# Two buffers for the keys of a differential attention, a tile of their own for the sample keys, and a smaller DMA scratch

## The chip, the core and the metric

The kernel runs on one core of one Trainium2 chip. TensorE (PE) multiplies matrices, VectorE (DVE), ScalarE (ACT) and GpSimd (POOL) do the rest, and SyncE (SP) issues every transfer of the program on one queue. The metric is the device time of one execution in microseconds, the median of the runs shown.

## The reference

One step of a one-layer hybrid encoder on a prompt of 2048 tokens and a sample of 32 tokens with a cache of 128 past tokens. All data is float32; the width is 1024.

```python
qa, ka, va, qb, kb, vb = split_proj(rmsnorm(hp, g_attn[i]), w_in[i])
oa = diff_attn_prompt(qa, ka, va, t5_table, lam)        # 4 heads, two q/k maps of 64, values of 128
ob = band_attn_prompt(qb, kb, vb, band_table[i])        # 8 heads of 64, 8 chunks of 64 back
hp = hp + merge(oa, ob, subln_g[i], out_norm_b[i], w_out[i], lam_init)
hp = ffn_ple(hp, p_prompt[i], g_mlp[i], w_up[i], w_down[i], w_ple_gate[i], w_ple_proj[i])
...
def diff_core(q, k, v, bias, mask, lam):
    s = jnp.einsum('bqhmd,bkhmd->bhmqk', q, k).astype(jnp.float32) * (HEAD_DIM ** -0.5) + bias[:, None]
    s = jnp.where(mask, s, NEG)
    p = jax.nn.softmax(s, axis=-1)
    w = p[:, :, 0] - lam * p[:, :, 1]
    return jnp.einsum('bhqk,bkhe->bqhe', w.astype(v.dtype), v)
```

The sample goes through the same layer; its keys in the differential attention are the 128 cached ones and its own 32. The mask is causal by chunks of 64 tokens. The outputs are both hidden states after a last norm, and the new keys and values.

## The kernel before

Large products are done in float32r in three terms: each operand is split into a rounded part and the rest (`split`, line 160 on; `mm3`, lines 186 to 192), so that one product of two operands is three matmuls. Tokens go in four blocks of 512; the last one takes the 32 sample tokens along.

Queries, keys and values are projected first (`proj`) and written to DRAM: `qS`, `kS`, `vS`. `kS` holds for each head the 2048 prompt keys, then 128 cached, then 32 sample keys: 2208 columns (`KC`), as a rounded part and a rest. The attention reads them back.

`attn_a` is the differential attention. It is called with a list of query pairs `js`; pair j is the 256 queries from 256 j on, and 8 stands for the sample. The calls are `JA0 = [(0, 1), (2, 3)]` early, in the pool `a0` (`self.small`, key tiles of 1024 columns), and `JA1 = [(4, 5), (6, 7, 8)]` later, in the pool `a1`. Each call goes over four heads g. For each head it loads

- a bias tile `ba` (`bias_a`, one buffer, with a memset on GpSimd for the mask),
- a key tile `ka` (one buffer): for each of two halves of the partitions, pieces of 1024 columns, so 2, 4 or 6 transfers,

and then runs the pairs (`attn_a_pair`). A pair loads its query tile `q` (`load_q`, two buffers, four transfers), and for each of its two 128-query tiles computes scores `s` with two matmuls (line 567) per key block of up to 512 columns and map, takes the maximum on VectorE (line 573, or with the bias line 576), the exponential on ScalarE (line 581), combines the two maps (lines 603, 604), transposes the weights on TensorE (`tpp`, line 639) and multiplies them with the values `v` (`o`, lines 653 to 655). `ka`, `ba` and `q` of the next head or pair can be loaded into a buffer only when the last reader of its old contents is done.

Nothing of the order is written by hand: a scheduler of the framework orders all instructions of each engine at build time, by program order as priority and by its own model of times and of free buffers. So work of other stages stands between the instructions of the attention: the projections of the band attention in the first stage, and in the second the output projection, the MLP (`ups`, `dps`) and the gate of the first two token blocks. Those run while `a1` is open because their tiles and those of `a1` lie side by side in SBUF. SP issues transfers strictly in its order and waits before each for what that transfer needs.

At address 0 of SBUF, 16384 bytes of each partition are set aside by default as scratch for dynamic DMAs (`dynamic_dma_scratch_size`); all pools lie behind it.

Of the kernel before, what the change touches and what calls it, by code (L numbers as in the profile page):

```python
# [13 lines left out]
F32R = mybir.dt.float32r  # L14
# [5 lines left out]
P = 128  # L20
D = 1024
SP = 2048
SS = 32
T = SP + SS
PAST = 128
KC = SP + PAST + SS
# [107 lines left out]
class Kern:  # L134
# [376 lines left out]
    def attn_a(self, js, pool, ps_s, ps_t, ps_o):  # L511
        nc = self.nc
        last = 8 in js
        nk = KC if last else 256 * (js[-1] + 1)
        for g in range(4):
            ba = self.bias_a(pool, g)
            kt = pool.tile([P, 2, 1024 if self.small else KC], F32R, tag="ka", bufs=1, name="ka")
            for hl in range(2):
                src = self.kS[g, hl].rearrange("(m r) c -> r m c", m=2)
                for c0 in range(0, nk, 1024):  # L520
                    c1 = min(c0 + 1024, nk)
                    self.dma(kt[64 * hl : 64 * hl + 64, :, c0:c1], src[:, :, c0:c1])
            for j in js:
                self.attn_a_pair(g, j if j < 8 else None, kt, ba, pool, ps_s, ps_t, ps_o)

    def attn_a_pair(self, g, j, kt, ba, pool, ps_s, ps_t, ps_o):
        nc = self.nc
# [7 lines left out]
        q = self.load_q(pool, g, t0, nq, (0, 1))  # L535
        ws = []
        for qi, t in enumerate(tiles):
            if samp:
                nr = SS
                blocks = [(SP, PAST + SS, 0)]  # L540
                kb = SP
                nkeys = PAST + SS
            else:
                nr = P
                kb = 0
                nkeys = P * (t + 1)
                nfar = max(nkeys - 256, 0)
                nb = (nfar + 511) // 512
                blocks = []
                pos = 0  # L550
                for i in range(nb):
                    n = P * ((nfar // P - pos // P + nb - i - 1) // (nb - i))
                    blocks.append((pos, n, None))
                    pos += n
                blocks.append((nfar, nkeys - nfar, 256 - (nkeys - nfar)))
            nb = len(blocks)
            e = [
                pool.tile([P, 2048 if not self.small else 1024], F32, tag=f"e{m}", bufs=2 if m == 0 or self.small else 1, name="e")
                for m in range(2)
            ]  # L560
            nm = pool.tile([P, 2, 8], F32, tag="nm", bufs=2, name="nm")
            z = pool.tile([P, 2, 8], F32, tag="z", bufs=2, name="z")
            for bi, (k0, n, near) in enumerate(blocks):
                for m in range(2):
                    s = ps_s.tile([P, 512], F32, tag="s", name="s")[:nr, :n]
                    for hl in range(2):
                        nc.tensor.matmul(  # L567
                            s, q[:, m, hl, P * qi : P * qi + nr], kt[:, m, k0 : k0 + n], start=hl == 0, stop=hl == 1
                        )
                    dst = e[m][:nr, k0 - kb : k0 - kb + n]  # L570
                    nmx = nm[:nr, m, bi : bi + 1]
                    if near is None:
                        nc.vector.tensor_reduce(nmx, s, axis=AX.X, op=ALU.max, negate=True)  # L573
                        src = s
                    else:
                        nc.vector.tensor_tensor_reduce(
                            dst, s, ba[:nr, near : near + n], 1.0, -3e38, ALU.add, ALU.max, nmx
                        )
                        nc.vector.tensor_scalar(nmx, nmx, -1.0, None, op0=ALU.mult)
                        src = dst  # L580
                    nc.scalar.activation(dst, src, AF.Exp, bias=nmx, accum_out=z[:nr, m, bi : bi + 1])  # L581
            c = pool.tile([P, 2, 8], F32, tag="c", bufs=2, name="c")
            rz = pool.tile([P, 2], F32, tag="rz", bufs=2, name="rz")
            if nb > 1:
                gm = pool.tile([P, 2], F32, tag="gm", bufs=2, name="gm")
                nc.vector.tensor_reduce(gm[:nr], nm[:nr, :, :nb], axis=AX.X, op=ALU.min)
                for m in range(2):
                    nc.scalar.activation(
                        c[:nr, m, :nb], nm[:nr, m, :nb], AF.Exp, bias=gm[:nr, m : m + 1], scale=-1.0
                    )  # L590
                nc.vector.tensor_tensor(z[:nr, :, :nb], z[:nr, :, :nb], c[:nr, :, :nb], op=ALU.mult)
                nc.vector.tensor_reduce(rz[:nr], z[:nr, :, :nb], axis=AX.X, op=ALU.add)
                nc.vector.reciprocal(rz[:nr], rz[:nr])
                nc.vector.tensor_scalar(c[:nr, 0, :nb], c[:nr, 0, :nb], rz[:nr, 0:1], None, op0=ALU.mult)
                nc.vector.tensor_scalar(
                    c[:nr, 1, :nb], c[:nr, 1, :nb], rz[:nr, 1:2], self.nlam[:nr], op0=ALU.mult, op1=ALU.mult
                )
            else:
                nc.vector.reciprocal(c[:nr, :, 0], z[:nr, :, 0])
                nc.vector.tensor_scalar(c[:nr, 1, 0:1], c[:nr, 1, 0:1], self.nlam[:nr], None, op0=ALU.mult)  # L600
            for bi, (k0, n, near) in enumerate(blocks):
                sl = slice(k0 - kb, k0 - kb + n)
                nc.scalar.activation(e[1][:nr, sl], e[1][:nr, sl], AF.Copy, scale=c[:nr, 1, bi : bi + 1])
                nc.vector.scalar_tensor_tensor(
                    e[0][:nr, sl], e[0][:nr, sl], c[:nr, 0, bi : bi + 1], e[1][:nr, sl], op0=ALU.mult, op1=ALU.add
                )
            ws.append(e[0])
# [7 lines left out]
        for c0 in range(0, len(kts), 4):  # L615
# [16 lines left out]
            for qi, w in enumerate(ws):  # L632
                nr = SS if samp else P
# [14 lines left out]
            for x, (i, kn) in enumerate(ch):  # L648
# [3 lines left out]
                last = c0 + x == len(kts) - 1  # L652
# [653 lines left out]
```

## Time and profile before

| | |
|---|---|
| runs | 3277.6, 3271.13, 3279.51 us |
| median | 3277.6 us |
| profiled execution | 3282.74 us |
| its span, first to last instruction | 3281.0 us |
| mean granted TensorE clock | 0.974 |
| first stage of `attn_a`, 230 to 560 us | PE busy 304.8 of 330 us |
| second stage of `attn_a`, 1331 to 2131 us | PE busy 762.2 of 800 us |

A row such as `PE s L567 <- DMA ka<-kS: 10.9, 5, 4.2` says that PE stood idle before the matmul of line 567 that writes `s`, until a transfer into `ka` had landed: 10.9 us in 5 cases, the longest 4.2 us. In a timeline, a row gives start, length, engine, line, operation, output and inputs, and in brackets the idle time before it with what ended it. In a table of windows each engine has its busy time and number of instructions; the last three columns are the granted clock, the busy share of the DMA engines and what they moved in GB/s.

### The profile page before, as it was taken

The page shows a single profiled execution, that of the slowest core. Times are in us where ns is not written, and L with a number is a line of the kernel's source. Part 1 is how long each engine was busy: PE and PEld are TensorE (multiplying, and loading weights), DVE is VectorE, ACT ScalarE, POOL GpSimd, SP SyncE. Part 2 cuts the span into 40 slices and gives each one's busy share as a digit, 9 for nine tenths or more (in the row PEclk, how much of TensorE's full clock was granted, in tenths as well). Part 3 has the DMA queues.
Part 4 walks back from the last instruction along what each step waited for, and adds up shares of the span by engine and source line. Part 5 has one row for each costly group of instructions (what it writes and reads, how often), then busy time and mean ns, then how long its engine had stood idle before and what let it go on. Part 6 is the DMA issues. An engine that isn't in the chain of part 4 may idle for free.

```text
span 3281.0 us, 51609 instructions
## 1 busy us (share of the span) xinstructions
PE 3096.6 (94%) x17881; PEld 2713.4 (83%) x17881; DVE 1562.2 (48%) x3952; ACT 1696.1 (52%) x3717; POOL 1711.0 (52%) x2515
## 2 busy tenths in 40 slices
PE   6998999899989999999999999998989999999998
PEld 6877788899877888778788877877779999999988
DVE  5116786444455544566655655735442232223235
ACT  4226676666656766666665656744442222222245
POOL 5436776433335544656654644676954333333377
PEclk9998999999999999999999999999989999999999
DMA  7488886876778654545655355357531111111123
GB/s 230 169 258 241 226 246 199 230 225 199 221 210 240 166 140 120 159 137 152 195 136 142 109 139 139 111 159 227 164 102 49 46 46 50 45 48 46 46 91 106
DMA packets 519085, 489.03 MB, mean 149 GB/s; under 512 B 37884, under 2 KB 414016, under 8 KB 518824
## 3 DMA queue, kind: packets, MB, share of 16 engines
q1 hardware_dynamic: 518824, 485.73, 50.8%
q8 instruction: 142, 2.33, 0.3%
q14 instruction: 119, 0.97, 0.1%
HBM read 379.06 MB, written 110.49 MB: 149 GB/s over the span
## 4 chain that ended last, share of the span: by engine, by line
PE 54%; DMA 5%; DVE 4%; POOL 2%; ACT 1%; issue 1%; SPq 0%; DVEq 0%; POOLq 0%; ACTq 0%
PE dps L190 7%; PE ups L191 7%; PE ups L190 7%; PE ups L192 7%; PE dps L192 7%; PE dps L191 7%; PE s L567 2%; PE gps L190 1%; PE gps L191 1%; DMA ka<-kS 1%; PE gps L192 1%; PE tpp L639 1%; POOL wl L164 1%; DMA wr<-w_up 1%; PE ob L766 1%
## 5 line engine op out<-in xcount | busy, mean ns | idle before, releaser
L164 POOL TENSOR_TENSOR wl<-wr,wh 128x256 fp32r<-128x256 f32 x936 | 690.9, 770 | 501.1 <-ACT wh L169 473.0
L971 DVE TENSOR_TENSOR h<-h,dps 128x512 f32<-128x512 f32 (+1 forms) x640 | 373.1, 585 | 597.5 <-PE dps L192 584.9
L169 ACT ACTIVATE wh<-wr 128x1024 fp32r<-128x1024 f32 x338 | 356.9, 1056 | 581.0 <-PE dps L191 285.7
L154 POOL TENSOR_TENSOR wl<-wr,wh 128x256 fp32r<-128x256 f32 x416 | 305.0, 764 | 407.0 <-ACT wh L169 403.7
L190 PE MATMUL dps<-uh,wh 128*128 128x512 f32 (+1 forms) x1280 | 458.6, 358 | 10.1 <-DVE h L971 5.5
L190 PE MATMUL ups<-cH,wh 128*128 128x512 f32 (+1 forms) x1280 | 453.3, 354 | 9.9 <-ACT relu L936 5.0
L191 PE MATMUL ups<-cL,wh 128*128 128x512 f32 (+1 forms) x1280 | 452.9, 354 | 4.1 <-DVE cL L175 3.6
L192 PE MATMUL ups<-cH,wl 128*128 128x512 f32 (+1 forms) x1280 | 453.2, 354 | 0.0
L191 PE MATMUL dps<-ul,wh 128*128 128x512 f32 (+1 forms) x1280 | 451.0, 353 | 0.0
L192 PE MATMUL dps<-uh,wl 128*128 128x512 f32 (+1 forms) x1280 | 450.9, 353 | 0.0
L154 POOL TENSOR_TENSOR ul<-relu,uh 128x136 fp32r<-128x136 f32 (+1 forms) x320 | 201.7, 652 | 167.7 <-ACT uh L169 166.4
L190 PEld LDWEIGHTS ups<-cH,wh 128*128 128x128 f32 x1280 | 242.8, 190 | 42.3 <-ACT relu L936 5.3
L190 PEld LDWEIGHTS dps<-uh,wh 128*128 128x128 f32 x1280 | 242.5, 189 | 42.4 <-DVE h L971 9.0
L191 PEld LDWEIGHTS ups<-cL,wh 128*128 128x128 f32 x1280 | 243.3, 190 | 36.0 <-DVE cL L175 3.8
L192 PEld LDWEIGHTS dps<-uh,wl 128*128 128x128 f32 x1280 | 242.0, 189 | 33.7
L192 PEld LDWEIGHTS ups<-cH,wl 128*128 128x128 f32 x1280 | 243.1, 190 | 30.1
L191 PEld LDWEIGHTS dps<-ul,wh 128*128 128x128 f32 x1280 | 242.2, 189 | 26.2
L190 PE MATMUL qps<-aH,wh 128*128 128x512 f32 (+1 forms) x640 | 231.3, 361 | 8.6 <-ACT kr L432 3.4
L191 PE MATMUL qps<-aL,wh 128*128 128x512 f32 (+1 forms) x640 | 229.6, 359 | 0.0
L192 PE MATMUL qps<-aH,wl 128*128 128x512 f32 (+1 forms) x640 | 228.9, 358 | 0.0
L567 PE MATMUL s<-ka,q 128*128 128x256 f32 (+4 forms) x784 | 190.4, 347 | 26.6 <-DMA ka<-kS 10.9
L581 ACT ACTIVATE e<-s,nm 128x512 f32<-128x512 f32 (+3 forms) x256 | 155.1, 611 | 68.7 <-DVE nm L573 46.0
(218 smaller groups left out, 7118.3 us busy)
## 6 DMA issues: line engine op xcount, KB each, us to landing
wr<-w_up SPq DMA_DIRECT2D x96, 512.0 KB, 4.2
wr<-w_down SPq DMA_DIRECT2D x96, 512.0 KB, 3.7
wr<-w_in SPq DMA_DIRECT2D x74, 512.0 KB, 5.2
q<-qS SPq DMA_DIRECT2D x256, 128.0 KB, 4.2
v<-vSa SPq DMA_DIRECT2D x64, 512.0 KB, 4.0
ka<-kS SPq DMA_DIRECT2D x32, 512.0 KB, 7.7
wr<-w_out SPq DMA_DIRECT2D x32, 512.0 KB, 5.4
wr<-w_ple_gate SPq DMA_DIRECT2D x32, 512.0 KB, 4.3
```

Source lines behind the costliest of these rows:

```text
L154: nc.gpsimd.tensor_tensor(out[:, sl], a[:, sl], b[:, sl], op=op)
L164: nc.gpsimd.tensor_tensor(out[:, sl], a[:, sl], b[:, sl], op=op)
L169: nc.scalar.activation(hi, raw, AF.Copy)
L190: nc.tensor.matmul(ps, lh, rh, start=start and i == 0, stop=False)
L191: nc.tensor.matmul(ps, lh, rl, start=False, stop=False)
L192: nc.tensor.matmul(ps, ll, rh, start=False, stop=stop and i == n - 1)
L567: nc.tensor.matmul(s, q[:, m, hl, P * qi : P * qi + nr], kt[:, m, k0 : k0 + n], start=hl == 0, stop=hl == 1)
L581: nc.scalar.activation(dst, src, AF.Exp, bias=nmx, accum_out=z[:nr, m, bi : bi + 1])
L639: nc.tensor.transpose(tp[:kn, x, :nr], w[:nr, P * i : P * i + kn], self.ident[:nr, :nr])
L766: nc.tensor.matmul(o[:, qa:qb], vt, pt[:kn, i - kfirst, qa:qb], start=x == 0 and y == 0, stop=x == len(order) - 1 and y == 1,)
L971: nc.vector.tensor_tensor(hv, hv, ps, op=ALU.add)
```

## The change

The key tile `ka` of the differential attention has two buffers where it had one, and in the later stage 2048 columns where it had 2208. The 160 columns that the sample needs go into a small tile `ks` of their own with one buffer, loaded only in the call with the sample; the score matmul subtracts the block base `kb` (0 for prompt pairs, 2048 for the sample) from its column. The scratch for dynamic DMAs shrinks from 16384 to 1024 bytes of each partition. The bytes loaded for the keys are the same. The number of key transfers of a head stays: 2 or 4, and in the call with the sample 4 into `ka` and 2 into `ks` where there were 6 into `ka`.

```diff
     def attn_a(self, js, pool, ps_s, ps_t, ps_o):
         nc = self.nc
         last = 8 in js
-        nk = KC if last else 256 * (js[-1] + 1)
+        nk = SP if last else 256 * (js[-1] + 1)
         for g in range(4):
             ba = self.bias_a(pool, g)
-            kt = pool.tile([P, 2, 1024 if self.small else KC], F32R, tag="ka", bufs=1, name="ka")
+            kt = pool.tile([P, 2, 1024 if self.small else SP], F32R, tag="ka", bufs=2, name="ka")
+            if last:
+                ks = pool.tile([P, 2, PAST + SS], F32R, tag="ks", bufs=1, name="ks")
             for hl in range(2):
                 src = self.kS[g, hl].rearrange("(m r) c -> r m c", m=2)
                 for c0 in range(0, nk, 1024):
                     c1 = min(c0 + 1024, nk)
                     self.dma(kt[64 * hl : 64 * hl + 64, :, c0:c1], src[:, :, c0:c1])
+                if last:
+                    self.dma(ks[64 * hl : 64 * hl + 64], src[:, :, SP:KC])
             for j in js:
-                self.attn_a_pair(g, j if j < 8 else None, kt, ba, pool, ps_s, ps_t, ps_o)
+                self.attn_a_pair(g, j if j < 8 else None, kt if j < 8 else ks, ba, pool, ps_s, ps_t, ps_o)
...
                     for hl in range(2):
                         nc.tensor.matmul(
-                            s, q[:, m, hl, P * qi : P * qi + nr], kt[:, m, k0 : k0 + n], start=hl == 0, stop=hl == 1
+                            s, q[:, m, hl, P * qi : P * qi + nr], kt[:, m, k0 - kb : k0 - kb + n], start=hl == 0, stop=hl == 1
                         )
...
-    nc = bacc.Bacc("TRN2", target_bir_lowering=False, num_devices=1)
+    nc = bacc.Bacc("TRN2", target_bir_lowering=False, num_devices=1, dynamic_dma_scratch_size=1024)
```

## The prediction

> **What bounds the kernel now.** I read the page first, then the waits of PE by stage, then the timeline around the longest waits, then the granted clock in those stretches.
>
> ```profile
> PE 3096.6 (94%) x17881; PEld 2713.4 (83%) x17881; DVE 1562.2 (48%) x3952; ACT 1696.1 (52%) x3717; POOL 1711.0 (52%) x2515
> ```
>
> PE is the bound: 184 us of the 3281.0 us span are without a matmul. The change touches no matmul (17,876 in the built program before and after), so all it can move is those idle stretches and the slower clock after them. The differential attention has two stages: 230 to 560 us (key blocks up to 1024, below "the first stage") and 1331 to 2131 us ("the second stage"). Between its softmax steps the scheduler has put projection matmuls in the first and MLP matmuls in the second. The waits of PE in the second stage (us in total, times, longest):
>
> ```profile
> PE s L567 <- DMA ka<-kS: 10.9, 5, 4.2
> PE s L567 <- issue: 7.2, 2, 4.9
> PE dps L190 <- DVE h L971: 5.5, 6, 1.6
> PE o L653 <- ACT pH L646: 4.5, 4, 2.3
> ```
>
> The score matmuls (line 567) lead the list. The two rows called "issue" are the same wait: both stand at the first score matmul of a head, right behind its key loads. Here is one, on PE and then on SP's queue:
>
> ```profile
> 1893.52 0.28 PE L653 MATMUL o<-pH,v 128*128 128x256 f32 x1
> 1898.72 1.19 PE L567 MATMUL s<-ka,q 128*128 128x512 f32 x2 [4.92 <-issue]
> 1899.71 0.63 PE L190 MATMUL ups<-cH,wh 128*128 128x512 f32 x1
> ```
>
> ```profile
> 1889.55 0.62 SPq L145 DMA_DIRECT2D ka<-kS  x1
> 1890.21 6.06 SPq L145 DMA_DIRECT2D q<-qS  x4
> ```
>
> The one key buffer is free only when the last score matmul of the head before is done; here six key loads and four query loads are then issued, and PE runs out of other matmuls before they land. The seven head changes of the second stage show one such gap each, in order 4.16, 2.29, 0.80, 2.44, 2.51, 4.92 and 0.94 us: 18.1 us, which is 10.9 + 7.2. In the first stage no PE wait names `ka`.
>
> The matmul after the gap takes 0.63 us, where the same shape takes 0.39 to 0.40 before it. The windows from the start of the three costliest gaps to the end of the halved clock (length, PE busy, ..., granted clock, DMA share, GB/s):
>
> ```profile
> 1416.44:1426.73 10.29, 6.13 (x18) 5.13 (x19) 7.40 (x13) 1.61 (x3) 2.55 (x4) 0.67 0.86 199
> 1779.36:1785.12 5.76, 3.25 (x11) 2.80 (x11) 0.69 (x1) 0.79 (x2) 1.40 (x2) 0.70 1.09 201
> 1893.80:1904.60 10.80, 5.88 (x14) 4.66 (x15) 2.31 (x7) 1.31 (x3) 2.77 (x4) 0.68 1.07 226
> ```
>
> All PE work in these windows runs after the gap, at half clock, so half of it is lost: (6.13 + 3.25 + 5.88) / 2 = 7.6 us. Two more key gaps (2.44 and 0.94 us) have a half-clock stretch a little later, but another wait (2.06 and 2.34 us) lies between; 1.7 us each, 3.4 us, I leave to the low end of the range.
>
> **Keys in two buffers: what goes.** In the order of the built program I counted the PE work between the matmul that frees a key buffer and the first score matmul that reads the new keys, at 0.23 us for 128x512 (start to start in the timeline) and in proportion for less. Before, in the second stage, it was 4.6 to 11.4 us at the seven head changes, against landings of the key loads of
>
> ```profile
> DMA to landing us min/median/max: 3.6/7.7/12.3
> ```
>
> After, it is 69 to 117 us there, and 15 to 50 us in the first stage. Even the 12.3 us maximum is covered. So 18.1 us of gaps and 7.6 us of half clock go: -25.7 us. That the other matmuls there are the cover is seen in the count itself; no PE work is added in their place.
>
> **What is late next, second stage.** The other inputs of a head's first score matmul are its query tile, two buffers, four loads of 0.60 us issue each. At the four head changes without a sample block the count between release and use is above 40 us: nothing. At the three that follow the sample block, the buffer comes free only with the last prompt scores of the head before, and the sample block is short: 4.5, 4.2 and 4.5 us, where before it was 15.0, 11.2 and 15.0. The landings of query loads in this stage:
>
> ```profile
> DMA to landing us min/median/max: 2.1/3.9/11.8
> ```
>
> The third load is needed and is issued 1.3 us after the first: 1.3 + 3.9 = 5.2 us at the median, 0.8 us more than the cover, so about 1 us at each change, +3 us. The bounds are 0 and 1.3 + 11.8 - 4.4 = 8.7 us each. I take the median because 11.8 belongs to query loads that stood behind a key burst, and that burst now stands behind them in SP's order. The two sample-key loads of a head carry 160 columns; their one buffer is free after the sample block and their use is above 100 us away, so they cost their issue, 2 x 0.6 us on SP, off the path. At the second of the three changes they stand between the second and third query load; that is within the 3 us.
>
> At the start of the second stage the first keys had 14.0 us of cover and have 11.4; in the trace the first score matmul came 12.3 us after the first key load was issued (1331.7 to 1344.0). Between 0 and 2.6 us; I take +1. Behind those loads on SP now stand the next head's keys, then the attention-output loads and weights of the output projection, as before.
>
> **What is late next, first stage.** The bias tile `ba` keeps one buffer. Its reload waits for VectorE's last use in the head before, and while keys were late too this hardly mattered. Counted in the same way, up to the first matmul that can't run without the biased scores, the cover at the seven head changes is 9.6, 6.3, 7.4, 13.5, 15.8, 3.3 and 9.4 us (before 11.2, 8.2, 4.3, 13.2, 12.6, 18.6 and 13.6). The loads there take
>
> ```profile
> DMA to landing us min/median/max: 2.2/5.1/10.5
> ```
>
> and the masking memset 0.14 us and the add 0.42 us come after: 5.7 us at the median, and some 0.8 us for VectorE to get to the release, my estimate from the two adds in front. So 6.5 us is needed; 3.3 us of cover leaves a gap of 3.2 us, 6.3 us leaves 0.2, and the 3.2 us gap costs 1.7 us of clock (5.76 us at 0.70, above): +5 us. Bounds: 0 (the 4.3 us case before shows no gap above 0.84 us next to it) and, at 10.5 us landings, the second rival below.
>
> **The rest.** The scratch size: the profile has every program transfer on one queue, and nothing of it is issued by POOL, so I cost it at nothing:
>
> ```profile
> q1 hardware_dynamic: 518824, 485.73, 50.8%
> ```
>
> The addresses move, but the attention tiles of the second stage still start 704 bytes above the MLP's tiles that run beside them (before 1728), so no new wait for space. The first 1,234 matmuls and the last 5,432 come in the same order; between them the scheduler has reordered, the same work with the same counts of short covers within a few, and I give that 0, with 5 us either way.
>
> **Sum.** -25.7 + 3 + 1 + 5 = -16.7 us. The profiled execution took 3282.74 us (span 3281.0), 5.1 us above the median; on the median, 3277.6 - 16.7 = 3261 us.
>
> **A rule of the skill.** The trace's row: the 2.51 us gap at 1779.36 is followed by a half-clock window of its own. By the Trainium skill, "TensorE: Matmul & The Clock Gate", Part 1, the clock falls after an idle window of about 3.4 us. By that only the 4.16 and 4.92 us gaps cost clock, 6.0 us in place of 7.6, and a 3.2 us gap in the first stage costs none, so the sum would be -16.8. The measurement differs on the short gap, and the sum goes by it.
>
> **The rivals.** First, nothing is gained: PE has other matmuls and some other wait fills the gaps, as the 5.5 us before `dps` and 4.5 us before `o` do now. For it: only 38 of the stage's 800 us are idle, and the order of what follows a gap changes. Against it: 18.1 of these 38 us stand at exactly the matmul whose cover grows tenfold. 3278 us; chance 0.08.
>
> Second, the bias tile: with all seven loads at 10.5 us, 11.1 us are needed, and the gaps are 1.5, 4.8, 3.7, 0, 0, 7.8 and 1.7 = 19.5 us, with 1.7 us of clock after five of them 28 us: 3277.6 - 25.7 + 4 + 28 = 3284 us. For it: DMA share there is 0.83. Against: the median of 5.1. Chance 0.12.
>
> Third, slower: the query loads after the sample blocks land as late as they did behind key bursts, now because SP holds them behind the sample-key loads, which wait for the sample's scores. 8.7 us at each of three changes, and 3.4 us of clock each (10.29 us at 0.67, above): 36 us, so 3277.6 - 25.7 + 36 + 1 + 5 = 3294 us. It decides from 6.6 us a change on. For it: the order at the second change. Against it: 0.16 MB stand there in place of 2.3 MB. Chance 0.08.
>
> Fourth, the smaller scratch slows each transfer; at 0.1 us for each of 1,639 issues SP gets 164 us more to do, and if a sixth shows, 3289 us. Against it is the queue row above; chance 0.03. The Trainium skill ("DMA: Bandwidth & Descriptors", SWDGE vs HWDGE vs iDMA) puts that scratch on the software path alone.
>
> **The numbers.** The forecast has 0.64; a larger gain 0.05 (no new waits and the 3.4 us as well: -29 us, 3248). A measurement can tell about 0.3%, 10 us. Faster: 0.62 of the forecast and the 0.05, 0.67. Within 0.3%: 0.02 of the forecast, 0.10 of the bias, 0.07 of nothing gained, 0.19. Slower: the rest of these, 0.03, with the third and fourth, 0.14. The range runs from 3246, the larger gain with a little reordering, to 3281, most of the bias case; about 0.2 is outside.
>
> **What would show it.** Right: in the second stage no PE wait on `ka`; at the three changes after a sample block waits of about 1 us on query loads; half-clock stretches near 1420, 1782 and 1898 us gone; in the first stage one gap of about 3 us behind a bias load. Wrong: idle PE time in 1331 to 2131 us still near 38 us, or over 10 us more of it in 230 to 560 us.

## The result: 12 us faster, and the profile after

The changed kernel takes 3265.2 us (median of 12 executions, 3258.5 to 3269.9), the kernel before 3277.3 us in the same round: a ratio of 0.9959, with a 95% interval from 0.9948 to 0.997. That is 12.0 us less; the forecast was 16.7 us less. The profiled execution after took 3263.55 us (span 3261.7, granted clock 0.980, before 0.974). The changed lines push the code down by 4: the score matmul is line 571 now, the residual add `h` line 975, the `o` matmuls lines 657 to 659.

The engine line of the page after: PE is busy 13.5 us less with the same number of matmuls, so part of the gain is clock.

```profile
PE 3083.1 (95%) x17881; PEld 2699.8 (83%) x17881; DVE 1549.0 (47%) x3952; ACT 1693.7 (52%) x3717; POOL 1709.8 (52%) x2515
```

The waits of PE in the second stage, 1331 to 2131 us, after (us in total, times, longest):

```profile
PE dps L190 <- DVE h L975: 8.3, 13, 1.3
PE s L571 <- DMA q<-qS: 3.7, 2, 2.8
PE s L571 <- ACT e L585: 3.2, 2, 2.1
PE o L657 <- ACT pH L650: 2.8, 3, 1.9
PE tpp L643 <- DVE e L608: 2.6, 2, 2.0
```

No row names `ka`, and "issue" behind it is gone too: all 18.1 us of key gaps have left. The list is not simply shorter, though. The MLP's wait for `h` rose from 5.5 us in 6 cases to 8.3 us in 13, `tpp` from 0.3 to 2.6 us, and the query tile is on it, as forecast.

SP's queue shows why no key is late. These are the four key loads of the last head, after; its first score matmul comes at 1992.7 us, over 100 us later:

```profile
1886.43 1.91 SPq L145 DMA_DIRECT2D q<-qS  x3
1888.38 2.55 SPq L145 DMA_DIRECT2D ka<-kS  x4
```

Both waits on query loads in the PE timeline after:

```profile
1347.81 2.71 PE L571 MATMUL s<-ka,q 128*128 128x512 f32 x6 [2.75 <-DMA q<-qS]
...
1766.58 0.70 PE L571 MATMUL s<-ka,q 128*128 128x512 f32 x2 [0.93 <-DMA q<-qS]
```

The first is at the start of the second stage, the second at one of the three head changes after a sample block; at the other two there is no wait.

Both stages as windows (length, PE, PEld, DVE, ACT and POOL busy, granted clock, DMA share, GB/s), before:

```profile
230.00:560.00 330.00, 304.81 (x1846) 269.30 (x1845) 230.82 (x720) 216.62 (x621) 221.59 (x314) 0.95 0.83 235
1331.00:2131.00 800.00, 762.21 (x3843) 641.30 (x3841) 497.85 (x1106) 511.86 (x1178) 446.79 (x623) 0.98 0.52 144
```

and after:

```profile
230.00:560.00 330.00, 294.36 (x1687) 254.96 (x1686) 224.08 (x716) 216.05 (x619) 213.57 (x302) 0.93 0.77 224
1331.00:2131.00 800.00, 771.76 (x3929) 646.30 (x3929) 502.63 (x1122) 513.50 (x1194) 447.07 (x628) 0.99 0.52 145
```

In the second stage PE's idle time falls by 9.6 us and the clock rises. In the first it grows from 25.2 to 35.6 us, but 159 matmuls fewer run in that window: the scheduler has put them elsewhere. So windows of fixed times compare different work, and a measure is needed that does not.

**A measure that follows the work.** I cut each trace at the first and last score matmul of the two stages and at the start of the last 5,432 matmuls, whose order is the same in all kernels; the last part ends with the last matmul. For each form of matmul I took what it costs undisturbed (the 40th percentile of the distance from one start to the next, over the twelve traces of this study). The length of a part less the undisturbed cost of its matmuls is its lost time: idle PE and slow clock together. The undisturbed cost of all matmuls comes to 2966 us in every kernel. The lost time in us:

| kernel | start | first stage | between | second stage | after it | last 5,432 | sum |
|---|---|---|---|---|---|---|---|
| before | 47.2 | 48.5 | 77.1 | 59.4 | 41.1 | 29.1 | 302.4 |
| before, small scratch (e1) | 51.2 | 43.8 | 79.6 | 63.0 | 40.0 | 27.1 | 304.7 |
| small tile alone (e8) | 49.8 | 46.8 | 84.3 | 52.2 | 40.1 | 21.0 | 294.1 |
| **after** | 49.6 | 63.2 | 59.6 | 46.7 | 40.7 | 23.2 | 283.0 |
| after, again (e5) | 48.2 | 63.2 | 71.3 | 43.9 | 41.2 | 22.9 | 290.7 |
| second stage alone (e2) | 47.7 | 49.4 | 76.5 | 48.1 | 39.4 | 20.9 | 282.0 |
| again (e6) | 49.9 | 44.0 | 69.0 | 47.8 | 39.6 | 21.0 | 271.3 |
| first stage alone (e3) | 51.6 | 62.1 | 67.9 | 61.6 | 45.9 | 20.9 | 310.0 |
| again (e7) | 50.3 | 63.7 | 66.6 | 61.3 | 43.8 | 23.0 | 308.7 |
| after, two bias tiles (e4) | 47.6 | 51.3 | 76.0 | 47.7 | 42.7 | 23.1 | 288.4 |
| after, three store tiles (e9) | 47.1 | 55.3 | 71.1 | 50.5 | 35.8 | 28.2 | 288.1 |
| after, both (e10) | 47.3 | 43.6 | 85.5 | 43.2 | 38.5 | 23.4 | 281.4 |

Where a kernel was profiled twice, or the order is the same, the columns show how far one execution can be trusted: within some 5 us in most places, 8 to 12 us in "between", and in the last 5,432 matmuls up to 8 us with the same order. The profiled executions of before and e1 were also 5.5 and 6.3 us above the medians of their rounds, those of e6 and e10 6.8 and 6.2 us below. So a single cell carries some us of chance, and the verdicts below rest on the medians of many executions.

### The profile page after: what moved, and what is told of

Same layout as the page of the kernel before. It is cut to its first block, busy times and chain, and to the rows that moved or that the text cites. A ratio compares the mean times of both kernels' runs of the same rounds, so it can differ in the third digit from the quotient of the medians.

```text
span 3261.7 us, 51605 instructions
## 1 busy us (share of the span) xinstructions
PE 3083.1 (95%) x17881; PEld 2699.8 (83%) x17881; DVE 1549.0 (47%) x3952; ACT 1693.7 (52%) x3717; POOL 1709.8 (52%) x2515
## 3 DMA queue, kind: packets, MB, share of 16 engines
q8 instruction: 142, 2.33, 0.3%
## 5 line engine op out<-in xcount | busy, mean ns | idle before, releaser
L190 PEld LDWEIGHTS dps<-uh,wh 128*128 128x128 f32 x1280 | 241.6, 189 | 47.2 <-DVE h L975 15.0
L571 PE MATMUL s<-ka,q 128*128 128x512 f32 (+3 forms) x768 | 189.8, 348 | 20.8 <-ACT e L585 10.4
```

What stands on the lines that cost most here:

```text
L190: nc.tensor.matmul(ps, lh, rh, start=start and i == 0, stop=False)
L571: nc.tensor.matmul(s, q[:, m, hl, P * qi : P * qi + nr], kt[:, m, k0 - kb : k0 - kb + n], start=hl == 0, stop=hl == 1)
```

## The experiments

Ratios are to the kernel before, on the same chip and in the same round, with 95% intervals. Those rounds gave the kernel before 3277.7 us (e1 to e4), 3276.5 (e5 to e8) and 3276.2 us (e9, e10).

### e1: the small scratch alone

```diff
-    nc = bacc.Bacc("TRN2", target_bir_lowering=False, num_devices=1)
+    nc = bacc.Bacc("TRN2", target_bir_lowering=False, num_devices=1, dynamic_dma_scratch_size=1024)
```

> The kernel before with the scratch for dynamic DMAs at 1024 bytes and nothing else; every engine has the same order of instructions, only addresses move. My theory (the scratch is not used by these transfers): same time, ratio 1.000 within 0.15%, and the seven key gaps at the head changes of the second stage stay, about 18 us in sum. Rival (the scratch slows each transfer): at 0.1 us for each of 1,639 issues, SP's own waits and the landings of key loads rise (7.7 us median before), and the time is 0.3% or more above before.

Measured: 3278.9 us, 1.0002 [0.9988, 1.0017]. The order on every engine is that of before, and its key waits in the second stage are those of before:

```profile
PE s L567 <- DMA ka<-kS: 11.3, 5, 5.0
PE s L567 <- issue: 9.3, 2, 6.1
```

So the scratch size costs and brings nothing, and the fourth rival falls. It also shows that the 18.1 us of key gaps in the profile of before are 20.6 us in another execution.

### e8: the small sample tile with one key buffer

```diff
-            kt = pool.tile([P, 2, 1024 if self.small else SP], F32R, tag="ka", bufs=2, name="ka")
+            kt = pool.tile([P, 2, 1024 if self.small else SP], F32R, tag="ka", bufs=1, name="ka")
```

(against the changed kernel)

> The sample keys in their small tile and the scratch at 1024, but one key buffer in both stages. Its order is that of before up to matmul 7,556 and for the last 7,122. My theory (the second key buffer makes the gain): the seven key gaps of the second stage are there with 15 to 20 us in sum, ratio 1.000 within 0.2%. Rival (the small tile or the new order makes the gain): ratio 0.997 or less.

Measured: 3273.0 us, 0.9992 [0.9982, 1.0002]. Its waits in the second stage:

```profile
PE s L571 <- DMA ka<-kS: 7.3, 3, 5.2
PE s L571 <- DMA q<-qS: 6.5, 2, 3.7
PE s L571 <- issue: 6.5, 2, 4.5
```

The small tile alone frees the key tile a sample block earlier and takes some of the key gaps away, but query waits appear in their place, and the time stays the same within the interval. The gain of the change needs the second key buffer: e6 below, run in the same round, differs from e8 by that buffer in the second stage alone and took 3258.6 us, 14.4 us less. The table does not split this cleanly: in the one trace of e8 the second stage already loses some 9 us less than before, and the part ahead of it some 6 us more.

### e2 and e6: two key buffers in the second stage alone

```diff
-            kt = pool.tile([P, 2, 1024 if self.small else SP], F32R, tag="ka", bufs=2, name="ka")
+            kt = pool.tile([P, 2, 1024 if self.small else SP], F32R, tag="ka", bufs=1 if self.small else 2, name="ka")
```

(against the changed kernel)

> Two key buffers and the small sample tile in the second stage alone; in the first stage the key tile keeps one buffer (scratch 1024). Its order is that of the kernel before up to matmul 7,572 and that of the changed kernel for the last 8,760. My theory (the second stage gains its 18 us of gaps and 8 to 12 us of clock, less some 4 us of new waits on queries; the first stage loses about 5 to 10 us with two buffers): 20 us below before, ratio 0.993 to 0.995, faster than the changed kernel by 3 to 8 us. Rival (the first stage costs nothing, the gain of the second is what is small): the same as the changed kernel, 0.996.

> Two key buffers and the sample tile in the second stage alone, again. My theory: 0.995, 2 to 6 us below both together. Rival (first stage free): equal to both together within 1 us.

Measured: 3262.5 us, 0.9951 [0.9936, 0.9966], and again 3258.6 us, 0.9946 [0.9934, 0.9959]: 15.3 and 17.9 us less than before; 20 us was expected of e2. This is the best version of the study, clearly so in the second round only (see e5). Its second stage loses 48 us where before lost 59 and 63, though it has a wait at its start that is shorter in the changed kernel. In e6, on SP, ScalarE and PE:

```profile
1334.22 4.42 SPq L145 DMA_DIRECT2D ka<-kS  x4
1338.69 1.25 SPq L145 DMA_DIRECT2D ks<-kS  x2
1339.99 1.06 SPq L145 DMA_DIRECT2D oraw<-oT  x2
...
1349.82 0.63 ACT L818 ACTIVATE sqacc<-oraw 128x512 f32<-128x512 f32 x1 [8.68 <-DMA oraw<-oT]
...
1353.53 1.22 PE L571 MATMUL s<-ka,q 128*128 128x512 f32 x2 [7.01 <-ACT e L585]
```

The keys of the next head are now free to be loaded early, and six of their transfers stand ahead of the attention-output loads that ScalarE needs now. ScalarE does nothing else in these 8.68 us, so the softmax behind line 818 is late too, and PE stands for 7.0 us. Both executions of this kernel show it (6.9 us in e2). The changed kernel has the same chain, with less idle time:

```profile
1354.01 4.55 SPq L145 DMA_DIRECT2D oraw<-oT  x4
...
1363.90 0.63 ACT L818 ACTIVATE sqacc<-oraw 128x512 f32<-128x512 f32 x1 [4.45 <-DMA oraw<-oT]
...
1366.65 0.66 PE L643 MATMUL tpp<-ident,e 128*128 128x128 f32 x4 [1.99 <-DVE e L608]
```

Its six key loads are issued from 1347.94 us on, ahead of these. Before, no key load of the next head stood there, and ScalarE waited 1.01 us for `oraw`.

### e3 and e7: two key buffers in the first stage alone

```diff
-            kt = pool.tile([P, 2, 1024 if self.small else KC], F32R, tag="ka", bufs=1, name="ka")
+            kt = pool.tile([P, 2, 1024 if self.small else KC], F32R, tag="ka", bufs=2 if self.small else 1, name="ka")
```

(against the kernel before, with the small scratch and no small tile)

> Two key buffers in the first stage alone; the second stage keeps one key tile of 2208 columns for all (scratch 1024). My theory: slower than before by 5 to 10 us, ratio 1.0015 to 1.003, idle PE in the first stage up from 25 to about 35 us; the key gaps of the second stage stay at about 18 us. Rival: no difference, 1.000.

> Two key buffers in the first stage alone, again. My theory: 1.004 again; of it some 5 us in the stretch before the second stage, some 5 to 10 us from the second stage to the MLP of the last two blocks, whose order differs from that of before although its buffers are the same. Rival: all of it lies before the second stage.

Measured: 3293.0 us, 1.0045 [1.0032, 1.0059], and again 3288.9 us, 1.0033 [1.002, 1.0045]: 15.2 and 12.4 us more. So the two halves of one edit have opposite signs. The first stage loses 62 to 64 us in place of 44 to 48, the part between 67 in place of 77 to 80: some 6 us more together. Another 4 us are lost after the second stage, whose buffers are those of before and whose order is not (44.9 us on average, before and e1 40.6). That is the split that was expected of e7, and its rival, all of it ahead of the second stage, fits less well, but both parts are no larger than the spread of single traces.

### e5: the changed kernel again, beside both halves

> The changed kernel once more, beside the two halves of the change on the same chip, for the sum of the parts: early alone gave 1.0045 to before, late alone 0.9951, and both together 0.9959. If the parts simply add, both would be 0.9996. My theory (the first stage costs about 5 us wherever it is done; the rest of what early alone lost is the second stage's new order around its key gaps): 0.996 again, and in the new trace the stretch from the first score matmul to the first of the second stage is about 5 us longer than with one buffer there. Rival (early costs 15 us by itself, and the late half gains 27): late alone beside it would be 0.992.

Measured: 3269.1 us, 0.997 [0.9958, 0.9981], a little above the first round. Taken with the first round the change brings 7.4 to 12.0 us. In the round of e5 and e6 the second buffer of the first stage costs 3269.1 - 3258.6 = 10.5 us on top of the second stage's; by the first round of each, which were two rounds on two chips, it costs 15.3 - 12.0 = 3.3 us, and there the intervals overlap. The rival's 0.992 for the late half did not come (e6: 0.9946). The 5 us that the theory expected ahead of the second stage can't be told from the table: from the first score matmul to the first of the second stage the changed kernel loses 122.8 and 134.5 us, the five traces with one buffer there 113.0 to 131.1 us.

### e4, e9 and e10: taking away the late tiles of the first stage

In the first stage the profile after has two long waits of PE that before has not. The first is behind the bias tile, on VectorE and then on PE:

```profile
453.26 0.42 DVE L580 CUSTOM_DVE_ANT_0 e<-s,ba 128x256 f32<-128x256 f32 x1 [2.52 <-POOL ba L293]
...
453.75 1.22 PE L571 MATMUL s<-ka,q 128*128 128x512 f32 x2 [2.33 <-DVE nm L580]
```

In the other trace of the same kernel (e5) VectorE does not wait for the bias tile at this place, and PE waits 0.62 us. The second is behind the store tile `os` of the attention output, on SP, ScalarE and PE; e5 has it too, with 3.37 us on PE:

```profile
325.59 0.39 SPq L145 DMA_DIRECT2D oT<-os  x1
...
335.93 0.38 ACT L661 ACTIVATE os<-o 128x256 f32<-128x256 f32 x1 [3.44 <-DMA oT<-os]
...
337.30 0.79 PE L571 MATMUL s<-ka,q 128*128 128x256 f32 x2 [3.54 <-ACT e L585]
```

This store is issued as soon as VectorE has written the tile (at 325.56 us), and ScalarE is released 10.3 us later. Query, key and weight loads were issued in the 7 us ahead of it; that these make it land late is argued, not tested. Waits of ScalarE on such a store are not new: before has 3.81 us at 360.1 us, but no gap of PE follows there. The window around the gap of PE runs at a granted clock of 0.62:

```profile
331.00:344.50 13.50, 8.03 (x34) 6.99 (x35) 6.76 (x28) 7.56 (x31) 6.40 (x11) 0.62 0.65 173
```

e4 gives the bias tile a second buffer in the first stage, e9 the store tile a third, e10 does both:

```diff
-        t = pool.tile([P, 256], F32, tag="ba", bufs=1, name="ba")
+        t = pool.tile([P, 256], F32, tag="ba", bufs=2 if self.small else 1, name="ba")
...
-        os_ = pool.tile([P, 256], F32, tag="os", bufs=2, name="os")[:, :nq]
+        os_ = pool.tile([P, 256], F32, tag="os", bufs=3 if self.small else 2, name="os")[:, :nq]
```

> The changed kernel with two buffers for the bias tile in the first stage. My theory (the bias load is late at the head changes there): the idle time of VectorE before the biased add that GpSimd's memset of the bias tile ends (3.4 us in the changed kernel, 230 to 560 us) goes, the 2.3 us PE gap near 451 us with its 1.7 us of clock goes too, and the time falls by 2 to 5 us, ratio to before 0.9945. Rival (the first stage is late for another reason, such as the output tile os, whose store held ScalarE for 3.4 us near 332 us): PE idle in the first stage stays near 35 us and the ratio stays 0.996.

> The changed kernel with a third buffer for the output tile os in the first stage. In four traces with two key buffers there, ScalarE stands 3.4 to 3.6 us near 332 us until an earlier store of os has landed, PE has a gap of 3.4 to 3.8 us behind it and 10.2 us of half clock follow. My theory (this wait is the larger part of what the first stage loses): gap and half clock go, from the first to the last score matmul of that stage about 8 us less idle and clock, ratio to before 0.994. Rival (with no slack left on ScalarE and VectorE there, the next late tile takes its place): no change, 0.996 to 0.997.

> The changed kernel with two bias tiles and three output tiles in the first stage. My theory (both late tiles are removed, so the first stage costs no more than with one key buffer): 0.994 to 0.995, as with the late half alone. Rival (the first stage with two key buffers is denser in softmax work than its engines can follow, whatever the tiles): 0.996 to 0.997, with the idle and clock of PE before the second stage unchanged.

Measured: e4 3268.7 us, 0.9968 [0.9957, 0.998]; e9 3272.4 us, 0.9986 [0.9976, 0.9996]; e10 3268.3 us, 0.9973 [0.9963, 0.9983]. None is faster than the changed kernel (0.9959 and 0.997), so none of the three theories came true; the rivals' 0.996 to 0.997 fit e4 and e10, and e9 lies above. The waits themselves did go: in e10 none of either kind is left. The first stage and the part between it and the second stage, in the changed kernel:

```profile
245.80:552.40 306.60, 274.16 (x1581) 238.54 (x1581) 215.63 (x695) 205.30 (x596) 199.96 (x282) 0.93 0.77 222
552.40:1347.80 795.40, 759.48 (x4764) 677.39 (x4762) 383.15 (x1278) 499.63 (x1032) 350.80 (x549) 0.99 0.69 196
```

and in e10:

```profile
243.47:531.26 287.79, 266.05 (x1587) 232.94 (x1586) 214.63 (x689) 204.12 (x591) 199.30 (x282) 0.95 0.82 237
531.26:1351.74 820.48, 772.09 (x4758) 686.21 (x4757) 382.20 (x1285) 500.43 (x1038) 349.96 (x550) 0.97 0.67 190
```

With almost the same matmuls in each part, e10's first stage is 18.8 us shorter and the part behind it 25.1 us longer. By the table the first stage and the part behind it lose 129.1 us together in e10 and 122.8 and 134.5 us in the two traces of the changed kernel. The late tiles are real waits, but removing them did not move the end of these 1,100 us.

## Why the prediction was right, and where it was off

**What goes: right.** All seven key gaps are gone. Of the half clock after them, forecast at 7.6 us, the stretches near 1420, 1782 and 1898 us are gone. By the table the second stage loses (59.4 + 63.0) / 2 = 61.2 us before and (46.7 + 43.9) / 2 = 45.3 us after, 15.9 us less. Of these, 11.8 us are idle PE (length less PE busy of that part: 34.5 us before and 38.1 us in e1, 24.4 and 24.7 us after), and some 4 us are clock, although up to 1.7 us of a new half clock at the start of the stage are in it. Both traces before are of executions above their medians, so part of this may be chance.

**What failed: the size of that term.** The sum let 25.7 us go and put 3 us of query waits in their place: 22.7 us. The runs show 15.9 us in the changed kernel and 13.2 us in the second stage alone. The working priced what is late next at the head changes only, and took the other waits of the stage as they are. But they grew. The key gaps were 18.1 and 20.6 us, 19.4 us on average, and idle PE fell by only 11.8 us: some 7.6 us came back, 0.9 us of it on query loads, 2.8 us at `dps` behind `h` (5.5 to 8.3 us), 2.3 us at `tpp` (0.3 to 2.6 us). In e2 and e6 it is for the most part one wait of 7 us behind the early key loads. One step of the working was wrong there: it let the attention-output loads stand on SP "as before" and put them at nothing. Before, no key load of the next head stood ahead of them. Now six do, ScalarE waits 4.45 us for them in place of 1.01 us, and the wait of 1.99 us at `tpp` hangs on that. In the changed kernel this adds little to PE's idle time, since before PE stood 3.12 us near 1353.7 us, behind ScalarE's wait of 5.04 us for weights; in e2 and e6 it costs the 7 us. The first rival, in which some other wait fills the gaps, had a chance of 0.08 as a whole; some 30% of it came true, as the 6.8 us missing from 22.7.

**Query loads after the sample blocks: smaller.** Three waits of about 1 us were forecast; there is one, 0.93 us. The landings of query loads in this stage fell from a median of 3.9 us to

```profile
DMA to landing us min/median/max: 2.1/3.0/8.4
```

and 1.3 + 3.0 = 4.3 us is about the cover of 4.2 to 4.5 us. At the one change that waits, a store stands on SP between the second and the third query load, and the third is issued 2.2 us after the first. The third rival, which decided from 6.6 us, is out.

**Start of the second stage: larger.** +1 us was forecast with bounds of 0 and 2.6 us; the wait is 2.75 us, on the query tile behind the keys, and 3.41 us of half clock follow, up to 1.7 us more.

**First stage: the sum came out near, the mechanism only in part.** The one bias gap is there in one trace of two: 2.33 us on PE at the change that had a cover of 3.3 us, where 3.2 us was forecast; in e5 it is 0.62 us, and not on the bias tile. The late store of `os` was not foreseen; its 3.54 us on PE (3.37 us in e5) with the low clock around it cost more. The first stage loses 63.2 us in both traces, against 48.5 and 43.8, so 17 us more and not 5; the part behind it loses 65.5 us against 78.4, so 13 us less. Net that is +4 us, with a spread of as much, and that it meets the forecast's +5 us is luck: neither of the two numbers was forecast. By the medians the first stage's buffer costs 3.3 to 10.5 us when the second stage has its own, and 12 to 15 us alone. The prediction's own sign of being wrong, over 10 us more idle in 230 to 560 us, is met (25.2 to 35.6 us). As a test it was badly made, since the scheduler moved 164 matmuls of the first stage, 19 us of work, behind it; but cut by the work, too, idle PE in that stage rises from 24.3 to 32.4 us, so for the first stage the sign told the truth.

**The rest: within its 5 us.** The part after the second stage is unchanged (40.6 us before and e1, 41.0 after). The last 5,432 matmuls lose 5 us less in the traces after, and also less in e8, which is not faster; the same order gives 20.9 to 29.1 us, so nothing is put down to the change there.

**The bias-tile rival** (3284 us) is out: at most one of seven reloads holds PE for long, and e4 shows that removing it brings nothing.

**Two slips of the working.** The key landings of 3.6/7.7/12.3 us are those of both stages; in the second alone they are 5.2/8.2/12.3 us, and the argument goes by the maximum. The fourth rival's sum gives 3288 us and not 3289. Neither moves the forecast.

**The clock after short waits: right.** Here are two windows of the changed kernel in the second stage. The first begins behind PE waits of 1.99 and 1.17 us, the second behind one of 2.07 us, and their granted clock is 0.57 and 0.66:

```profile
1368.00:1376.00 8.00, 7.37 (x21) 5.95 (x22) 4.63 (x13) 7.52 (x19) 8.00 (x12) 0.57 0.35 87
1685.00:1690.00 5.00, 4.79 (x14) 3.75 (x15) 2.40 (x4) 4.67 (x13) 3.75 (x6) 0.66 0.31 109
```

So gaps of 2 us can cost clock here too, as the sum took it. Not each one does: behind the key gap of 2.29 us at 1499 us, before, a 128x512 matmul takes 0.39 to 0.40 us again, as it did ahead of the gap. The Trainium skill, "TensorE: Matmul & The Clock Gate", Part 1, speaks of an idle window of about 3.4 us; the measurement differs.

**What stays open.** Why the second buffer of the first stage costs time is not settled. It is neither of the two late tiles nor both (e4, e9, e10), no scratch (e1), and not the small tile (e3 and e7 have none). Lost time that e4, e9 and e10 remove from the first stage comes back before the second. What sets the length of these two parts together was not isolated; a candidate, not tried, is what the order of the band attention's softmax and of the projections does there.

## What to carry to other kernels

Price a second buffer stage by stage: the same `bufs=2` brought 15 to 18 us where a load at the head change was the longest wait of an otherwise well filled stage, and cost 12 to 15 us alone where it was not late in the first place (part of that, it seems, by the new order of later stages). Behind a removed wait look at the whole list of waits of that stage, not only at the next input of the same matmul; here some 30% of the gain went into other, mostly short waits. An early load is an early place in an in-order queue: list what it is now issued ahead of.

## What the runs showed of the hardware beyond expectation

The last 5,432 matmuls, in the same order in every kernel, lost 20.9 to 29.1 us from one execution to another, so stages of two single traces cannot be compared to better than some us. And the clock can fall before a long gap has lasted: in the changed kernel a half-clock stretch of 10.24 us begins at 334.0 us, 0.25 us into the gap of 3.54 us, behind three gaps of 0.6 to 0.7 us in the 3.6 us ahead of it.
